# Seven block products for each pair of gate and up blocks in the second block's feed-forward

## Chip, cores and metric

The kernel runs on one core of one Trainium2 chip. The metric is the device time of one execution in microseconds. The time before is the median of three runs.

## What is computed

Two transformer blocks in float32 on 512 tokens (528 with meta tokens in the first block) of width 1024. The change touches the feed-forward of the second block (`d_model` 1024, inner width 2816):

```python
n2 = rmsnorm(h, g_ffn)
h = h + (jax.nn.silu(n2 @ w_ffn_gate) * (n2 @ w_ffn_up)) @ w_ffn_down
```

The factor 1/rms of a token multiplies a whole column of the transposed products, so the kernel applies it behind the products and only the gain `g_ffn` ahead of them.

## The kernel before

Activations are kept transposed: a row block is a tile of 128 features by 512 tokens, eight of them make the 1024 features. A weight block is 1024 x 128, kept as a tile of 128 x 8 x 128.

Every float32 operand of a matmul is split in two parts (high and low, tiles of type float32r), and a product is three matmuls: high by high, high by low, low by high (`mm`, L237 to L239; the weights' tiles are `wh` and `wl`). `load_w` (L218) loads a block from HBM into `wr` by SyncE's queue, copies it to `wh` on ScalarE (ACT, L226) and subtracts on VectorE (DVE, L228) for `wl`; each of these tags has three buffers (pool `wp`). `split` (L262) does the same for activations, and `gain_split` (L282) with the gain in it. `one` (L1327) computes one output block of 128 x 512 into a PSUM bank that `bank` (L245) picks: 8 x 3 matmuls of 128 x 512.

The end of `block2` (L1376 to L1452) runs in this order: eight output projections with residual (L1378 to L1383), `rstd` and the broadcast of 1/rms into `rsbc` (L1385 to L1387), eight gain splits (L1388), then three groups of inner blocks (8, 8 and 6, the loop at L1389). In a group each inner block j takes one gate and one up product; each is multiplied by `rsbc` out of PSUM (L1397, L1399), the gate goes through Silu (L1398), their product (L1400) is split (L1401). Then eight down projections (L1403) sum the group into the residual H. The ending (L1404 on) is the gate of a per-layer embedding and the final norm.

```python
nc.vector.tensor_tensor(g1, self.one(self.load_w(A["w_ffn_gate"][j]), X), rs_bc, OP.mult)
nc.scalar.activation(g1, g1, AF.Silu)
nc.vector.tensor_tensor(g2, self.one(self.load_w(A["w_ffn_up"][j]), X), rs_bc, OP.mult)
```

The order in which an engine gets its instructions is set by the tile framework's scheduler when the program is built; each engine then works its own list in order and waits on semaphores. A tag with n buffers lets the next tile in only when the readers of the n-th last are done. TensorE is PE below, with PEld its weight loads, GpSimd is POOL, SyncE is SP.

## Time and profile before

| what | value |
|---|---|
| median of 3 runs | 2286.45 us (2282.49 to 2290.6) |
| profiled execution, its own time | 2280.83 us |
| its span | 2279.0 us |
| mean granted clock of TensorE | 0.98 |
| PE busy | 2175.6 us (95%) |
| DVE, ACT, POOL busy | 1196.4, 918.6, 437.8 us |
| instructions: PE, DVE, ACT, POOL | 12395, 2045, 1544, 835 |

The profiled execution is one of the program's executions, its span the time from the first instruction to the last. Matmuls overlap in the pipeline, so PE's busy share alone tells little; the starts of successive matmuls and the waits between them do. The second block's feed-forward lies from about 1830 to 2222 us: gate and up products, the eight down projections of a group, and again.

### The profile page before, as it was taken

The page shows a single profiled execution, that of the slowest core. Times are in us where ns is not written, and L with a number is a line of the kernel's source. Part 1 is how long each engine was busy: PE and PEld are TensorE (multiplying, and loading weights), DVE is VectorE, ACT ScalarE, POOL GpSimd, SP SyncE. Part 2 cuts the span into 40 slices and gives each one's busy share as a digit, 9 for nine tenths or more (in the row PEclk, how much of TensorE's full clock was granted, in tenths as well). Part 3 has the DMA queues.
Part 4 walks back from the last instruction along what each step waited for, and adds up shares of the span by engine and source line. Part 5 has one row for each costly group of instructions (what it writes and reads, how often), then busy time and mean ns, then how long its engine had stood idle before and what let it go on. Part 6 is the DMA issues. An engine that isn't in the chain of part 4 may idle for free.

```text
span 2279.0 us, 31959 instructions
## 1 busy us (share of the span) xinstructions
PE 2175.6 (95%) x12395; PEld 1897.2 (83%) x12395; DVE 1196.4 (52%) x2045; ACT 918.6 (40%) x1544; POOL 437.8 (19%) x835
## 2 busy tenths in 40 slices
PE   6888899999999998899999999999999999999998
PEld 5887888999999977688888888788788888888887
DVE  4665667644434577653443465554554454344355
ACT  4554565323323476542332443343443332232233
POOL 4233431693000222100000002880000000000001
PEclk8899999999999999999999999999999999999999
DMA  4111232244342244232222236224223332222222
GB/s 148 58 48 29 64 108 83 101 130 151 110 123 93 84 74 96 62 133 97 93 93 99 96 111 144 80 82 123 100 89 96 127 114 93 102 93 93 99 91 88
DMA packets 105872, 221.93 MB, mean 97 GB/s; under 512 B 27812, under 2 KB 46361, under 8 KB 105720
## 3 DMA queue, kind: packets, MB, share of 16 engines
q1 hardware_dynamic: 105720, 219.88, 31.0%
q8 instruction: 98, 1.61, 0.3%
q14 instruction: 54, 0.44, 0.1%
HBM read 202.91 MB, written 15.57 MB: 96 GB/s over the span
## 4 chain that ended last, share of the span: by engine, by line
PE 86%; DVE 6%; ACT 3%; DMA 2%; issue 2%; POOL 1%; SPq 1%; DVEq 0%; ACTq 0%
PE mm L237 14%; PE mm L238 14%; PE mm L239 13%; PE x L237 10%; PE x L239 10%; PE x L238 10%; PE s L237 1%; PE s L238 1%; PE s L239 1%; PE s L662 1%; PE s L772 1%; PE t L390 1%; PE t L1042 1%; ACT wh L226 1%; PE s L1618 0%
## 5 line engine op out<-in xcount | busy, mean ns | idle before, releaser
L226 ACT ACTIVATE wh<-wr 128x1024 fp32r<-128x1024 f32 (+3 forms) x360 | 350.2, 974 | 1035.6 <-PE x L238 497.6
L228 DVE TENSOR_TENSOR wl<-wr,wh 128x1024 fp32r<-128x1024 f32 (+2 forms) x301 | 354.1, 1177 | 167.9 <-ACT wh L226 167.5
L237 PE MATMUL mm<-x,wh 128*128 128x512 f32 (+2 forms) x1144 | 409.8, 358 | 22.5 <-DVE raw L654 7.3
L238 PE MATMUL mm<-x,wh 128*128 128x512 f32 (+2 forms) x1144 | 404.3, 353 | 7.4 <-DVE x L287 7.4
L239 PE MATMUL mm<-x,wl 128*128 128x512 f32 (+2 forms) x1144 | 403.1, 352 | 0.0
L237 PEld LDWEIGHTS mm<-x,wh 128*128 128x128 f32 x1144 | 222.1, 194 | 52.8 <-ACT x L286 7.2
L237 PE MATMUL x<-x,wh 128*128 128x512 f32 (+1 forms) x728 | 258.3, 355 | 0.0
L239 PE MATMUL x<-x,wl 128*128 128x512 f32 (+1 forms) x728 | 257.4, 354 | 0.0
L238 PE MATMUL x<-x,wh 128*128 128x512 f32 (+1 forms) x728 | 257.1, 353 | 0.0
L238 PEld LDWEIGHTS mm<-x,wh 128*128 128x128 f32 x1144 | 221.7, 194 | 34.3 <-DVE x L287 8.5
L239 PEld LDWEIGHTS mm<-x,wl 128*128 128x128 f32 x1144 | 221.9, 194 | 28.1 <-issue 0.8
L228 POOL TENSOR_TENSOR wl<-wr,wh 128x1024 fp32r<-128x1024 f32 (+2 forms) x59 | 102.8, 1743 | 432.8 <-ACT wh L226 399.7
L237 PE MATMUL mm<-k,wh 128*128 128x272 f32 (+1 forms) x520 | 177.8, 342 | 1.2 <-ACT raw L892 0.5
L239 PE MATMUL mm<-k,wl 128*128 128x272 f32 (+1 forms) x520 | 176.4, 339 | 0.0
L238 PE MATMUL mm<-m,wh 128*128 128x272 f32 (+2 forms) x520 | 170.9, 329 | 5.7 <-DVE m L264 5.7
L239 PE MATMUL x<-k,wl 128*128 128x256 f32 (+1 forms) x520 | 174.3, 335 | 0.0
L237 PE MATMUL x<-k,wh 128*128 128x256 f32 (+1 forms) x520 | 173.6, 334 | 0.5 <-DVE h L880 0.5
L239 PEld LDWEIGHTS x<-x,wl 128*128 128x128 f32 x728 | 137.8, 189 | 20.1
L237 PEld LDWEIGHTS x<-x,wh 128*128 128x128 f32 x728 | 138.0, 190 | 19.5
L238 PEld LDWEIGHTS x<-x,wh 128*128 128x128 f32 x728 | 137.7, 189 | 19.8
L292 POOL TENSOR_TENSOR rs<-col,mhalf 128x5 f32<-128x5 f32 (+2 forms) x8 | 9.0, 1128 | 728.8 <-DVE col L304 728.8
L238 PE MATMUL x<-m,wh 128*128 128x256 f32 (+1 forms) x432 | 139.6, 323 | 0.1
(471 smaller groups left out, 3996.1 us busy)
## 6 DMA issues: line engine op xcount, KB each, us to landing
wr<-w_up SPq DMA_DIRECT2D x64, 512.0 KB, 3.3
wr<-w_down SPq DMA_DIRECT2D x64, 512.0 KB, 3.3
wr<-w_in SPq DMA_DIRECT2D x56, 512.0 KB, 3.2
wr<-w_ffn_gate SPq DMA_DIRECT2D x22, 512.0 KB, 3.3
wr<-w_ffn_up SPq DMA_DIRECT2D x22, 512.0 KB, 3.2
wr<-w_ine SPq DMA_DIRECT2D x18, 512.0 KB, 3.5
wr<-w_ffn_down SPq DMA_DIRECT2D x16, 512.0 KB, 3.3
wr<-w_ino SPq DMA_DIRECT2D x10, 512.0 KB, 3.2
```

Of the source, the lines that this page charges most:

```text
L226: nc.scalar.activation(wh, raw, AF.Copy)
L228: eng.tensor_tensor(wl, raw, wh.bitcast(F32), OP.subtract)
L237: self.nc.tensor.matmul(ps, wh[:, k0 + j], xh[:, a:b], start=start and j == 0, stop=False)
L238: self.nc.tensor.matmul(ps, wh[:, k0 + j], xl[:, a:b], start=False, stop=False)
L239: self.nc.tensor.matmul(ps, wl[:, k0 + j], xh[:, a:b], start=False, stop=stop and j == nk - 1)
L292: self.nc.gpsimd.tensor_tensor(dst, src, self.mhalf[:src.shape[0], :n], OP.pow)
L390: nc.tensor.transpose(t[:nk, b, :n], P[:n, k:k + nk], eye)
L662: nc.tensor.matmul(ps, v[:n, b], p[:n, b, :w], start=b == 0 and j == 0, stop=b == 4 and j == len(seq) - 1)
L772: self.nc.tensor.matmul(s[:, hf, :264], q, k[j][:, ks], start=j == 0, stop=j == 1)
L1042: nc.tensor.transpose(t[:, 128 * j:128 * j + 128], E[c][n][:, k:k + 128], self.turn)
```

## The change

Each pair of a gate block and an up block is now computed with a seven-product scheme for 2 x 2 block matrices (Strassen's, in the form with shared sums). The 2 x 2 blocks are: on the weights' side gate and up by even and odd K blocks (w11, w12 of the gate, w21, w22 of the up block), on the activations' side even and odd row blocks by the first and second 256 tokens. Each product has four K blocks and 256 columns: 4 x 3 matmuls of 128 x 256, into one half of a PSUM bank.

`seven_w` loads both blocks (the up block into the new tag `w2`), forms four sums of 128 x 512 on POOL into two tiles `ws`, and splits four tiles: the gate block, the two tiles of sums, and half of the up block. `seven_x` makes seven operands out of the eight row blocks with gain, once. `seven` runs the seven products and puts the results together on DVE, with two PSUM copies on ACT and one sum on POOL. The products with `rsbc` move from DVE (out of PSUM) to POOL (in SBUF). PSUM takes its banks from six in turn for the whole stage. The stage becomes a function `ffn` of its own, with a pool for the new tags (`x7` 8 buffers, `xo` 8, `ws` 3, `w2` 2, `st` 6).

```diff
@@ -227,6 +227,93 @@
         eng = nc.gpsimd if self.on_pool[self.nw % len(self.on_pool)] else nc.vector
         eng.tensor_tensor(wl, raw, wh.bitcast(F32), OP.subtract)
         return wh, wl
+
+
+    def seven_w(self, src1, src2):
+
+
+        nc = self.nc
+        self.n += 1
+        raws = self.wp.tile([128, 8, 128], F32, tag="wr", name=f"wr{self.n}", bufs=3), self.u("w2", F32, (128, 8, 128))
+        for raw, src in zip(raws, (src1, src2)):
+            nc.sync.dma_start(raw, src)
+        eo = lambda t: [t.rearrange("p (i e) n -> p e i n", e=2)[:, e] for e in range(2)]
+        (w11, w12), (w21, w22) = map(eo, raws)
+        s, r = self.u("ws", F32, (128, 8, 128)), self.u("ws", F32, (128, 8, 128))
+        G = nc.gpsimd
+        G.tensor_tensor(s[:, 0:4], w21, w22, OP.add)
+        G.tensor_tensor(s[:, 4:8], s[:, 0:4], w11, OP.add)
+        G.tensor_tensor(r[:, 0:4], w21, w11, OP.add)
+        G.tensor_tensor(r[:, 4:8], s[:, 4:8], w12, OP.add)
+        parts = []
+        for x, n in ((raws[0], 8), (s, 8), (r, 8), (w22, 4)):
+            self.n += 1
+            wh = self.wp.tile([128, 8, 128], F32R, tag="wh", name=f"wh{self.n}")
+            wl = self.wp.tile([128, 8, 128], F32R, tag="wl", name=f"wl{self.n}")
+            nc.scalar.activation(wh[:, :n], x, AF.Copy)
+            nc.vector.tensor_tensor(wl[:, :n], x, wh[:, :n].bitcast(F32), OP.subtract)
+            parts.append((wh, wl))
+        (ah, al), (sh, sl), (rh, rl), (dh, dl) = parts
+        (ah0, ah1), (al0, al1) = eo(ah), eo(al)
+        return ((ah0, al0), (ah1, al1), (sh[:, 0:4], sl[:, 0:4]), (sh[:, 4:8], sl[:, 4:8]),
+                (rh[:, 0:4], rl[:, 0:4]), (rh[:, 4:8], rl[:, 4:8]), (dh[:, 0:4], dl[:, 0:4]))
+
+    def seven_x(self, Z):
+
+
+        nc = self.nc
+        ops = [[] for _ in range(7)]
+        for i in range(4):
+            z0, z1 = Z(2 * i), Z(2 * i + 1)
+            A, B = slice(0, 256), slice(256, 512)
+            p, q = self.u("raw", F32, (128, 512)), self.u("raw", F32, (128, 512))
+            nc.vector.tensor_tensor(p[:, A], z0[:, A], z0[:, B], OP.subtract)
+            nc.vector.tensor_tensor(p[:, B], z1[:, B], z0[:, B], OP.subtract)
+            nc.vector.scalar_tensor_tensor(q[:, A], z1[:, B], -1.0, p[:, A], op0=OP.mult, op1=OP.subtract)
+            nc.vector.tensor_tensor(q[:, B], z1[:, A], q[:, A], OP.add)
+            h0, l0 = self.u("xo", F32R, (128, 256)), self.u("xo", F32R, (128, 256))
+            self.split(z0[:, A], h0, l0)
+            h1, l1 = self.split_new(z1, ("x", "x"))
+            hp, lp = self.split_new(p, ("x", "x"))
+            hq, lq = self.split_new(q, ("x7", "x7"))
+            for o, (h, l, c) in zip(ops, ((h0, l0, A), (h1, l1, A), (h1, l1, B), (hp, lp, A), (hq, lq, A), (hp, lp, B), (hq, lq, B))):
+                o.append((h[:, c], l[:, c]))
+        return ops
+
+    def seven(self, W, X, o1, o2):
+
+        nc = self.nc
+        w11, w12, s1, s2, r1, r2, w22 = W
+        b11, b21, b22, t1, t2, t3, t4 = X
+        A, B = slice(0, 256), slice(256, 512)
+
+        G = nc.gpsimd
+
+        def prod(w, x):
+            ps = self.bank()[:, A]
+            for j, (xh, xl) in enumerate(x):
+                nc.tensor.matmul(ps, w[0][:, j], xh, start=j == 0, stop=False)
+                nc.tensor.matmul(ps, w[0][:, j], xl, start=False, stop=False)
+                nc.tensor.matmul(ps, w[1][:, j], xh, start=False, stop=j == 3)
+            return ps
+
+        def new(ps=None):
+            t = self.u("st", F32, (128, 256))
+            if ps is not None:
+                nc.scalar.activation(t, ps, AF.Copy)
+            return t
+
+        v1 = new(prod(w11, b11))
+        nc.vector.tensor_tensor(o1[:, A], prod(w12, b21), v1, OP.add)
+        v2 = new()
+        nc.vector.tensor_tensor(v2, prod(s2, t2), v1, OP.add)
+        c5 = new(prod(s1, t1))
+        v3 = new()
+        nc.vector.tensor_tensor(v3, prod(r1, t3), v2, OP.add)
+        G.tensor_tensor(v2, v2, c5, OP.add)
+        nc.vector.scalar_tensor_tensor(o2[:, B], c5, -1.0, v3, op0=OP.mult, op1=OP.subtract)
+        nc.vector.tensor_tensor(o2[:, A], prod(w22, t4), v3, OP.subtract)
+        nc.vector.tensor_tensor(o1[:, B], prod(r2, b22), v2, OP.add)
 
     def mm(self, ps, w, xs, sl, ks=None, k0=0, start=True, stop=True):
 
@@ -1381,22 +1468,31 @@
             nc.vector.tensor_tensor(h, self.one(self.load_w(A["w_out"][m]), mix), x, OP.add)
             self.sq_add(acc, h, m == 0, (0, 512))
             H.append(h)
+        return H, acc
+
+    def ffn(self, H, acc):
+        nc, A = self.nc, self.A
 
         rs = self.rstd(acc, 1024, BLOCKS2)
         rs_bc = self.u("rsbc", F32, (128, 512))
         self.bcast(rs_bc, rs, BLOCKS2)
-        X = [self.gain_split(H[m], self.g(C_GF, m), (0, 512)) for m in range(8)]
+
+        def z(m):
+            t = self.u("q", F32, (128, 512))
+            nc.scalar.activation(t, H[m], AF.Copy, scale=self.g(C_GF, m))
+            return t
+
+        self.banks(6)
+        X = self.seven_x(z)
         for a, b, wd in ((0, 8, lambda m: A["w_ffn_down0"][0, m]), (8, 16, lambda m: A["w_ffn_down0"][1, m]),
                          (16, 22, lambda m: A["w_ffn_down1"][0, m])):
             S = []
             for j in range(a, b):
-                if j in (0, 2):
-                    self.banks(2 if j else 6)
-                g1, g2 = self.u("raw"), self.u("raw")
-                g1, g2 = g1[:, :512], g2[:, :512]
-                nc.vector.tensor_tensor(g1, self.one(self.load_w(A["w_ffn_gate"][j]), X), rs_bc, OP.mult)
+                g1, g2 = self.u("raw")[:, :512], self.u("raw")[:, :512]
+                self.seven(self.seven_w(A["w_ffn_gate"][j], A["w_ffn_up"][j]), X, g1, g2)
+                nc.gpsimd.tensor_tensor(g1, g1, rs_bc, OP.mult)
                 nc.scalar.activation(g1, g1, AF.Silu)
-                nc.vector.tensor_tensor(g2, self.one(self.load_w(A["w_ffn_up"][j]), X), rs_bc, OP.mult)
+                nc.gpsimd.tensor_tensor(g2, g2, rs_bc, OP.mult)
                 nc.vector.tensor_tensor(g1, g1, g2, OP.mult)
                 S.append(self.split_new(g1, ("k", "h")))
             for m in range(8):
@@ -1654,7 +1750,9 @@
                 return
             st.callback(self.inner.__exit__, None, None, None)
             with self.pool({"o2": 3, "pd": 2, "pf": 2, "dmask": 1}):
-                self.block2(*got)
+                got = self.block2(*got)
+            with self.pool({"x7": 8, "xo": 8, "ws": 3, "w2": 2, "st": 6}):
+                self.ffn(*got)
 
     def pool(self, tags):
         return self.sb.open(self.tc, tags)
```

**Order, the inner blocks.** DVE, one pair before the change (`raw` are the two results, `k` and `h` the split of the product, `mm` and `x` PSUM banks):

```order
L1397 TENSOR_TENSOR raw_19083<-mm_19091,rsbc_18068 128x512
L228 TENSOR_TENSOR wl_19192<-wr_19190,wh_19191 128x1024
L1399 TENSOR_TENSOR raw_19084<-x_19124,rsbc_18068 128x512
L1400 TENSOR_TENSOR raw_19083<-raw_19083,raw_19084 128x512
L228 TENSOR_TENSOR wl_19231<-wr_19229,wh_19230 128x1024
L264 TENSOR_TENSOR h_19152<-raw_19083,k_19151 128x512
```

DVE now, one period of a pair in the middle of a group. `wl<-ws` and `wl<-w` are low parts of the sums and of the up block's half, `wl<-wr` of the gate block of the pair after; `s`, `mm` and `x` are PSUM banks, `st` SBUF tiles:

```order
L254 TENSOR_TENSOR wl_18900<-ws_18889,wh_18899 128x1024
L316 TENSOR_TENSOR raw_18743<-s_18861,st_18800 128x256
L351 TENSOR_TENSOR h_18740<-raw_18603,k_18739 128x512
L254 TENSOR_TENSOR wl_18904<-ws_18890,wh_18903 128x1024
L307 TENSOR_TENSOR raw_18883<-mm_18926,st_18924 128x256
L254 TENSOR_TENSOR wl_18908<-w_18886,wh_18907 128x512
L309 TENSOR_TENSOR st_18940<-x_18941,st_18924 128x256
L254 TENSOR_TENSOR wl_19036<-wr_19025,wh_19035 128x1024
L312 TENSOR_TENSOR st_18970<-s_18971,st_18940 128x256
L1496 TENSOR_TENSOR raw_18743<-raw_18743,raw_18744 128x512
L314 SCALAR_TENSOR_TENSOR raw_18884<-st_18968,st_18970 128x256
L315 TENSOR_TENSOR raw_18884<-s_18987,st_18970 128x256
```

Six instructions became twelve; seven of the twelve read two SBUF tiles, five read a PSUM bank and an SBUF tile. The two that read PSUM and `rsbc` are gone.

**Order, POOL.** Before, POOL's list between the scan of the state-space part and the ending:

```order
L1505 TENSOR_TENSOR st_14638<-a_5053,vh_14000 64x32 x2
L1506 TENSOR_TENSOR st_14637<-st_14637,vh_14000 128x32
L1507 TENSOR_TENSOR vh_14000<-st_14637,st_14638 128x32
L292 TENSOR_TENSOR rs_18066<-col_18064,mhalf 128x4
L1431 TENSOR_SCALAR m_17795<-m_17795,cols 128x512
L1431 TENSOR_SCALAR m_17833<-m_17833,cols 128x512
```

The row of L292 is the 1/rms; nothing stands between it and the ending. POOL now, one period of a pair (`ws<-` are the four sums for a later pair, L1495 and L1493 the products with `rsbc` of an earlier pair, L313 a sum of the current one):

```order
L244 TENSOR_TENSOR ws_19169<-w_19166 128x512
L313 TENSOR_TENSOR st_18940<-st_18940,st_18968 128x256
L245 TENSOR_TENSOR ws_19169<-ws_19169,wr_19165 128x512
L1495 TENSOR_TENSOR raw_18884<-raw_18884,rsbc_18072 128x512
L246 TENSOR_TENSOR ws_19170<-w_19166,wr_19165 128x512
L247 TENSOR_TENSOR ws_19170<-ws_19169,wr_19165 128x512
L1493 TENSOR_TENSOR raw_18883<-raw_18883,rsbc_18072 128x512
```

Seven instructions per pair are new on this engine. Right behind these rows comes the end of the first group:

```order
L244 TENSOR_TENSOR ws_19565<-w_19562 128x512
L313 TENSOR_TENSOR st_19080<-st_19080,st_19108 128x256
L1495 TENSOR_TENSOR raw_19024<-raw_19024,rsbc_18072 128x512
L1493 TENSOR_TENSOR raw_19023<-raw_19023,rsbc_18072 128x512
L313 TENSOR_TENSOR st_19220<-st_19220,st_19248 128x256
L1495 TENSOR_TENSOR raw_19164<-raw_19164,rsbc_18072 128x512
L1493 TENSOR_TENSOR raw_19163<-raw_19163,rsbc_18072 128x512
L245 TENSOR_TENSOR ws_19565<-ws_19565,wr_19561 128x512
L246 TENSOR_TENSOR ws_19566<-w_19562,wr_19561 128x512
L244 TENSOR_TENSOR ws_19705<-w_19702 128x512
L247 TENSOR_TENSOR ws_19566<-ws_19565,wr_19561 128x512
```

The first row is a sum for the next group's first pair; the six behind it finish the group's last two pairs; from L245 on stand the rest of the eight sums for the next group's first two pairs. Eight such sums also stand ahead of the first group.

## Rows read from the trace of the kernel before

**Rows 1.** The page, chain that ended last: share of the span by engine.

```profile
PE 86%; DVE 6%; ACT 3%; DMA 2%; issue 2%; POOL 1%; SPq 1%; DVEq 0%; ACTq 0%
```

**Rows 2.** Busy us per engine, two stretches; PEclk, DMA share, GB/s.

```profile
core 0: us, PE busy (x) PEld busy (x) DVE busy (x) ACT busy (x) POOL busy (x), PEclk, DMA share, GB/s
627.00:684.00 57.00, 57.00 (x471) 56.91 (x470) 22.32 (x32) 14.06 (x16) 0.00 (x0) 1.00 0.41 121
1995.00:2052.00 57.00, 57.00 (x249) 46.56 (x248) 26.77 (x32) 17.70 (x22) 0.00 (x0) 1.00 0.27 93
```

**Rows 3.** PE's waits, 1830 to 2200 us: total us, times, longest us.

```profile
PE mm L237 <- DVE m L1403: 0.3, 1, 0.3
```

**Rows 4.** Timeline of PE (start us, us, instruction): first and last of 22.

```profile
1989.71 0.40 PE L239 MATMUL mm<-x,wl 128*128 128x512 f32 x1
...
1994.54 0.39 PE L239 MATMUL mm<-x,wl 128*128 128x512 f32 x1
```

**Rows 5.** Timeline of PE at 256 columns: first and last of 24.

```profile
743.75 0.28 PE L237 MATMUL x<-k,wh 128*128 128x256 f32 x1
...
746.46 0.28 PE L239 MATMUL x<-k,wl 128*128 128x256 f32 x1
```

**Rows 6.** DVE groups, 1760:2210 us: count, busy us, mean ns, idle before.

```profile
L228 DVE TENSOR_TENSOR wl<-wr,wh 128x1024 fp32r<-128x1024 f32 x72 | 88.1, 1223 | 19.6 <-ACT wh L226 19.5
L1400 DVE TENSOR_TENSOR raw<-raw,raw 128x512 f32<-128x512 f32 x22 | 15.2, 692 | 2.6 <-ACT raw L1398 0.7
L287 DVE SCALAR_TENSOR_TENSOR x<-m,cols,x 128x512 fp32r<-128x512 f32 x8 | 6.0, 746 | 0.0
L228 DVE TENSOR_TENSOR wl<-wr,wh 128x512 fp32r<-128x512 f32 x8 | 5.4, 681 | 0.0
```

**Rows 7.** ACT groups, same stretch.

```profile
L226 ACT ACTIVATE wh<-wr 128x1024 fp32r<-128x1024 f32 x72 | 76.4, 1061 | 248.2 <-PE mm L238 119.7 <-issue 80.8 <-PE x L238 43.6
L226 ACT ACTIVATE wh<-wr 128x512 fp32r<-128x512 f32 x7 | 4.4, 633 | 20.8 <-PE mm L238 12.4 <-PE x L238 8.4
```

**Rows 8.** POOL: one of 512 (timeline); four of 256 (ns min/median/max).

```profile
184.87 1.27 POOL L228 TENSOR_TENSOR wl<-wr,wh 128x512 fp32r<-128x512 f32 x1 [4.76 <-ACT wh L226]
...
L1449 POOL TENSOR_TENSOR k<-m,rsbc x4: 723/725/910, 2268.2 to 2273.2; 128x256 f32<-128x256 f32 x4
```

**Rows 9.** Timeline of DVE near the start.

```profile
8.92 0.77 DVE L287 SCALAR_TENSOR_TENSOR x<-m,cols,x 128x528 fp32r<-128x528 f32 x1 [0.41 <-ACT x L286]
9.61 0.70 DVE L512 TENSOR_TENSOR acc<-acc,raw 128x528 f32<-128x528 f32 x1
...
15.44 2.88 DVE L512 TENSOR_TENSOR acc<-acc,raw 128x528 f32<-128x528 f32 x1
18.24 2.84 DVE L287 SCALAR_TENSOR_TENSOR x<-m,cols,x 128x528 fp32r<-128x528 f32 x1
```

**Rows 10.** Timeline of POOL, same time: two of 1024 in one row.

```profile
14.99 5.53 POOL L228 TENSOR_TENSOR wl<-wr,wh 128x1024 fp32r<-128x1024 f32 x2
```

**Rows 11.** Timeline of DVE at 456 us.

```profile
456.41 0.42 DVE L1139 TENSOR_TENSOR h<-x,h 128x256 f32<-128x256 f32 x1 [2.38 <-PE x L239]
457.39 1.41 DVE L228 TENSOR_TENSOR wl<-wr,wh 128x1024 fp32r<-128x1024 f32 x1 [0.55 <-ACT wh L226]
```

**Rows 12.** Timeline of POOL, same time.

```profile
456.17 0.43 POOL L1243 TENSOR_TENSOR p<-p,p 128x128 f32<-128x128 f32 x1
...
457.29 0.43 POOL L1242 TENSOR_TENSOR p<-p,p 128x128 f32<-128x128 f32 x1
457.67 1.41 POOL L1243 TENSOR_TENSOR p<-p,p 128x128 f32<-128x128 f32 x1
```

**Rows 13.** A wait of PE; the stretch behind it (columns as rows 2).

```profile
1380.13 2.10 PE L1496 MATMUL s<-u,sw 128*128 128x64 f32 x10 [1.77 <-issue]
1380.20:1390.00 9.80, 9.80 (x40) 9.12 (x41) 3.18 (x4) 4.40 (x5) 0.00 (x0) 0.51 0.45 139
```

**Rows 14.** Timeline of DVE, output projections.

```profile
1827.84 0.69 DVE L1381 TENSOR_TENSOR m<-mm,raw 128x512 f32<-128x512 f32 x1 [2.13 <-PE mm L239]
```

## Prediction

> **What bounds the kernel now.** I read the chain of waits first: TensorE's matmuls make up 86% of what ended last [rows 1]. Then the busy time by stretch: in a stretch of gate and up projections (from 1995 us) PE is busy all 57 us at a granted clock of 1.00, while DVE is busy 26.77, ACT 17.70 and POOL 0.00 [rows 2]. Then PE's waits in the whole feed-forward stage of the second block: one, of 0.3 us [rows 3]. So this stage costs what its matmuls cost, and a change here is worth its matmuls only as long as no other engine becomes later than PE.
>
> The timeline gives the spacing of matmuls: 512 columns, 22 starts from 1989.71 to 1994.54, so 4.83/21 = 0.230 us [rows 4]; 256 columns, 24 starts from 743.75 to 746.46, so 2.71/23 = 0.118 us [rows 5]. PEld's records fill all of the stretch from 627 us, where 272 and 256 columns alternate [rows 2]; its loads are thus in that spacing already.
>
> **The change, part by part.** A pair is one gate block and one up block; there are 22.
>
> *Matmuls.* Removed per pair: 2 x 8 x 3 = 48 of 512 columns, 48 x 0.230 = 11.04 us. Added: 7 x 4 x 3 = 84 of 256 columns, 84 x 0.118 = 9.91 us. Alone that is -1.13 us a pair, -24.9 us in all.
> The page "TensorE: Matmul & The Clock Gate" of the Trainium skill (section "Back-to-back issue gap") speaks against such a trade: about 81 ns per matmul at 128 columns and 131 ns at 512 in a stream with weight loads. By a straight line between them, an estimate, 256 columns would take 98 ns, the pair 8.2 us in place of 6.3, and the stage 42 us more. The rows here show 0.118 and 0.230, nearly a half, and the measurement decides.
>
> *ACT* gets per pair 3 x 1.06 + 0.63 for the wh tiles [rows 7], two PSUM copies, a Silu and a split, none over 0.63: under 6.4 us, less than PE's 9.91, hidden by it. The DMAs carry the same bytes as before.
>
> *DVE* gets per pair twelve instructions. Seven read two SBUF tensors: three wl of 1024 elements (1.22 each), one of 512 (0.68), the product of gate and up (0.69), a split (0.69 at most) [rows 6] and the 256-wide L314 (about 0.42, as the 256-wide row of rows 11). That is 6.14 us. Five read PSUM, 0.42 each [rows 11]. Together 8.2 us: alone it would fit under 9.91.
>
> *POOL*, idle in this stage before, gets six instructions of 512 (1.27 each) and one of 256 (0.73) [rows 8]: 8.35 us. Alone it would fit too.
>
> *Together they don't fit.* At the start of the program a DVE instruction on 528 elements takes 0.70 or 0.77, but 2.88 and 2.84 while POOL runs two instructions of 1024 [rows 9, 10]. Subtract the usual length from the end: the first DVE row came through at 18.32 - 0.70 = 17.62, the second at 21.08 - 0.77 = 20.31. At 456 us it goes the other way: POOL's row at 457.67 takes 1.41 instead of 0.43, that is, it came through at 458.65, and the DVE row beside it, 1.41 instead of 1.22, at 457.58 [rows 11, 12]. One waits until the other is done. So a DVE instruction of 1024 elements holds POOL up for 458.65 - 457.58 = 1.07 us, and (528 elements: 0.55) POOL's 1024 hold DVE up from 18.17 to 20.31, 2.14 us. The DVE row at 456.41, which reads PSUM and one SBUF tensor, takes 0.42 in the middle of POOL's stream: it doesn't take part.
> The page "SBUF — State Buffer" of the Trainium skill (section "Who interferes with whom") says the same of a DVE instruction with two SBUF inputs and a GpSimd one that reads SBUF, and that the one that starts first keeps the port pair for its whole instruction. The rows agree on who waits, but show a hold a little shorter than the record. By the page's words the sum is nearer the upper bound below, by the rows nearer the lower one.
>
> The price per pair. Lower bound, holds end to end: POOL 6 x 1.07 + 0.54 = 6.96; DVE 3 x 1.07 + 3 x 0.54 + 0.27 = 5.10; 12.1 us. Upper bound, whole records end to end: 8.35 + 6.14 = 14.5 us. Both are over 11.04. I take 13.0, nearer the lower end, because the contested rows go by holds; the 0.9 above it is for moments in which one engine waits for data rather than for the other.
>
> PE has no slack to absorb this. The wh and wl tags have three buffers and a pair now takes four tiles: the next pair's second tile (in the order: raw gate block, s, r, half of the up block) gets the buffer of this pair's third, which the seventh product reads last. From that product's end ACT (1.06) and DVE (1.22) have 24 x 0.118 = 2.83 us, the next pair's first two products, to make it: 0.55 us to spare. One POOL instruction of 512 in front of that subtraction (1.07) uses it up, and the PSUM evictions queue behind it on DVE.
>
> Not every pair pays. The sums for the first pairs of a down-projection group are formed while the down projections or the output projection run (POOL has nothing else there), and beside the last two pairs of a group POOL forms hardly any sums for a following pair (its order, shown above with the change, has one sum of the next group there). I let two pairs in each of the three groups run at PE's 9.91: 6 x (9.91 - 11.04) = -6.8. The other 16: 16 x (13.0 - 11.04) = +31.4; bounds 16 x 1.06 = +17 and 16 x 3.46 = +55.
>
> *Operands.* The eight gain splits (DVE 8 x 0.75 = 6.0 [rows 6]) become 20 instructions of 256 (0.42) and 12 of 512 (0.69): 16.7 us of DVE, in four equal steps. Three steps lie beside the output projections, where DVE sits idle 2.13 us before an eviction [rows 14]; the last needs the last row block: 4.2 us against one split of 0.75 before. I take +4; bounds 0 and 16.7 - 6.0 = +10.7.
>
> Sum: -6.8 + 31.4 + 4 = **+28.6 us**. The profiled execution took 2280.83 us (span 2279.0) and would go to 2309; it lies 5.6 under the median of the runs shown, 2286.45, so the median would be **2315 us**. A difference under 0.3%, 7 us, can't be told from none by a measurement of this kernel.
>
> **The rivals.**
> *The port doesn't bind; PE does.* Then the stage gains 24.9 and loses 4 at the start: 2265 us. For it: each engine alone is under 9.91. Against: rows 9 to 12; it needs the port work to fall under 9.9 us a pair, and the lower bound is 12.1.
> *A draw.* If far more of the sums fall into the down projections than I grant, so that the 16 pairs average about 11.2, the result is 16 x 0.16 - 6.8 + 4 = 0: 2286. Against: ws has three buffers, one and a half pairs.
> *The clock falls as well.* Behind a PE wait of 1.77 us the granted clock averaged 0.51 over 10 us [rows 13], that is, it stood at 1.2 GHz nearly all the time, where the gate and up products have 2.4 GHz, 1.00 [rows 2]. A wait of about 3 us in each pair could do that 16 times. Much of the slower time lies under the same port work, so I price it with the port's upper bound: 55 - 6.8 + 10.7 = +59, 2345 us; a drop that isn't covered adds to that.
>
> **How the numbers follow.** Forecast 0.70; clock and upper bound 0.11; PE bound 0.11; a draw 0.08. The port's bounds with those of the operands give 17 - 6.8 + 0 = +10 to +59, 2296 to 2345. To hold 8 in 10 I go from 2290, within the draw, to 2348, and leave out the gain and the far end of the clock case. Slower by over 0.3%: 0.70 + 0.11 = 0.81; within: 0.08; faster: 0.11.
>
> **What would show it.** Right: 36 more matmuls per pair, 0.118 apart while they run; POOL's 512-wide records at about 2 us instead of 1.27 and DVE's wl at about 2 instead of 1.22; PE idle two to three us per pair, put down to DVE wl L254, some 45 us over the stage; the gate and up stretches longer, the down stretches the same. Wrong: PE busy throughout the pairs and DVE and POOL at their usual lengths (the gain came), or a 256-wide spacing well over 0.118 with no wait (the matmuls or the clock were the cause).

## The result and the profile after

| kernel | median us (lowest to highest) | ratio to before, 95% interval |
|---|---|---|
| before | 2284.47 (2278.04 to 2290.60, 4 runs) | |
| changed | 2315.45 (2303.09 to 2320.19, 4 runs) | 1.0128 [1.0079, 1.0177] |

The kernel became slower by 1.3%; 2315 was forecast. The profiled execution took 2320.19 us. The page, busy time and the chain that ended last [rows 1]:

```profile
PE 2170.4 (94%) x13187; PEld 1928.5 (83%) x13187; DVE 1361.1 (59%) x2201; ACT 972.7 (42%) x1648; POOL 690.4 (30%) x989
...
PE 75%; DVE 10%; POOL 5%; ACT 3%; DMA 3%; issue 3%; SPq 1%; DVEq 0%; ACTq 0%; POOLq 0%
```

PE's share of the chain fell from 86 to 75%; DVE and POOL gained 8 points. By the shares of busy time alone nothing seems short: DVE is busy 59% of the span and POOL 30%. The stage tells more. PE's waits in the second block's feed-forward (1810 to 2260 us; line and releaser, total us, times, longest), where one wait of 0.3 us had been [rows 3]:

```profile
PE s L297 <- DVE wl L254: 25.2, 17, 2.4
PE mm L297 <- DVE wl L254: 6.3, 4, 2.5
PE x L297 <- DVE wl L254: 3.3, 3, 1.2
```

All 34.8 us are waits for the low part of a weight tile, in 24 places. Busy time over the first five spacings of the second group, a spacing running from one pair's last eviction to the next pair's (columns as rows 2):

```profile
2026.52:2091.33 64.81, 56.36 (x432) 54.47 (x431) 58.40 (x59) 27.15 (x41) 57.96 (x35) 0.95 0.26 82
```

A pair takes 64.81/5 = 12.96 us there, in place of 11.04; that is a mean of 14.16, 10.47, 13.66, 14.14 and 12.38. DVE is busy 58.40 us of it, POOL 57.96, about 11.6 us a pair each, where their own work is 8.2 and 8.35. The groups of the same stretch (count, busy us, mean ns) show where the rest comes from; DVE, against rows 6 and 11:

```profile
L254 DVE TENSOR_TENSOR wl<-ws,wh 128x1024 fp32r<-128x1024 f32 x10 | 20.6, 2062 | 0.0
L254 DVE TENSOR_TENSOR wl<-wr,wh 128x1024 fp32r<-128x1024 f32 x5 | 9.8, 1968 | 0.0
L254 DVE TENSOR_TENSOR wl<-w,wh 128x512 fp32r<-128x512 f32 x5 | 7.2, 1439 | 0.0
...
L1496 DVE TENSOR_TENSOR raw<-raw,raw 128x512 f32<-128x512 f32 x5 | 4.8, 950 | 4.5 <-ACT raw L1494 4.5
...
L315 DVE TENSOR_TENSOR raw<-s,st 128x256 f32<-128x256 f32 x3 | 1.2, 409 | 0.0
```

POOL, against rows 8:

```profile
L1493 POOL TENSOR_TENSOR raw<-raw,rsbc 128x512 f32<-128x512 f32 x5 | 10.3, 2059 | 0.0
L246 POOL TENSOR_TENSOR ws<-w,wr 128x512 f32<-128x512 f32 x5 | 10.3, 2053 | 0.0
...
L313 POOL TENSOR_TENSOR st<-st,st 128x256 f32<-128x256 f32 x5 | 7.3, 1452 | 0.0
L245 POOL TENSOR_TENSOR ws<-ws,wr 128x512 f32<-128x512 f32 x5 | 7.0, 1392 | 0.1
L244 POOL TENSOR_TENSOR ws<-w 128x512 f32<-128x512 f32 x5 | 6.6, 1313 | 6.8 <-DMA w<-w_ffn_up 5.2 <-DVE raw L1496 1.5
```

DVE's low parts went from 1.22 to 2.06 and 1.97 us and from 0.68 to 1.44; POOL's 512-wide rows from 1.27 to as much as 2.06. DVE's instructions that read a PSUM bank and one SBUF tile stayed at 0.41. One such moment, in DVE's timeline (start, us, instruction):

```profile
1920.38 1.96 DVE L254 TENSOR_TENSOR wl<-ws,wh 128x1024 fp32r<-128x1024 f32 x1
```

in PE's (in brackets the idle time before it and what ended it):

```profile
1919.61 0.28 PE L296 MATMUL x<-x,wh 128*128 128x256 f32 x1
1922.39 0.39 PE L297 MATMUL mm<-x,wl 128*128 128x256 f32 x1 [2.50 <-DVE wl L254]
1922.61 0.28 PE L295 MATMUL mm<-x,wh 128*128 128x256 f32 x1
```

and the clock behind it (columns as rows 2):

```profile
1923.00:1926.50 3.50, 3.50 (x21) 3.50 (x20) 3.50 (x3) 0.50 (x1) 3.50 (x3) 0.56 0.00 0
```

The subtraction ended at 1922.34 and PE went on at 1922.39, 2.50 us late. A microsecond later the granted clock stood at 1.2 GHz for some 3.4 us. In half-microsecond slices there are five such falls in the stage, each 0.4 to 1.4 us behind a wait of 1.75 to 2.50 us; they cost 8.5 us of full-speed time together. Not every such wait has one behind it: one of 2.13 us, which ended at 1908.08, has none. The stage before has no fall.

**Length of the stage**, from the start of the first output-projection eviction to that of the last down eviction: 402.6 us before (1819.53 to 2222.1), 430.0 after (from 1831.75 to the second row here, DVE's timeline):

```profile
1831.75 0.69 DVE L1468 TENSOR_TENSOR m<-mm,raw 128x512 f32<-128x512 f32 x1 [4.04 <-PE mm L326]
...
2261.75 0.69 DVE L1499 TENSOR_TENSOR m<-s,m 128x512 f32<-128x512 f32 x1 [1.41 <-PE s L326]
```

So the stage grew by 27.4 us. The two profiled executions are 39.4 us apart: the stage starts 12.2 us later, after unchanged code (last section), and 0.2 come back behind it. The experiments are therefore read by the stage and the spacing of pairs beside the ratio.

### The profile page after: what moved, and what is told of

Read it like the earlier page. It is cut to its first block, busy times and chain, and to the rows that moved or that the text cites. A ratio compares the mean times of both kernels' runs of the same rounds, so it can differ in the third digit from the quotient of the medians.

```text
span 2318.4 us, 34040 instructions
## 1 busy us (share of the span) xinstructions
PE 2170.4 (94%) x13187; PEld 1928.5 (83%) x13187; DVE 1361.1 (59%) x2201; ACT 972.7 (42%) x1648; POOL 690.4 (30%) x989
## 4 chain that ended last, share of the span: by engine, by line
PE 75%; DVE 10%; POOL 5%; ACT 3%; DMA 3%; issue 3%; SPq 1%; DVEq 0%; ACTq 0%; POOLq 0%
PE mm L324 11%; PE mm L325 11%; PE mm L326 11%; PE x L325 8%; PE x L324 8%; PE x L326 8%; PE s L324 2%; PE s L325 2%; PE s L326 2%; DVE wl L254 2%; PE s L749 1%; PE s L859 1%; PE t L477 1%; DVE wl L228 1%; DMA w<-w_ffn_up 1%
## 5 line engine op out<-in xcount | busy, mean ns | idle before, releaser
L226 ACT ACTIVATE wh<-wr 128x1024 fp32r<-128x1024 f32 (+3 forms) x316 | 303.1, 961 | 838.4 <-PE x L325 469.1
L228 DVE TENSOR_TENSOR wl<-wr,wh 128x1024 fp32r<-128x1024 f32 (+2 forms) x257 | 323.2, 1259 | 156.9 <-ACT wh L226 156.0
L324 PE MATMUL mm<-x,wh 128*128 128x512 f32 (+2 forms) x976 | 344.8, 353 | 31.4 <-DVE h L1226 8.3
L325 PE MATMUL mm<-x,wh 128*128 128x512 f32 (+2 forms) x976 | 338.7, 347 | 7.4 <-DVE x L374 7.4
L326 PE MATMUL mm<-x,wl 128*128 128x512 f32 (+2 forms) x976 | 337.4, 346 | 0.0
L324 PEld LDWEIGHTS mm<-x,wh 128*128 128x128 f32 x976 | 191.0, 196 | 55.1 <-DVE h L1226 8.5
L325 PEld LDWEIGHTS mm<-x,wh 128*128 128x128 f32 x976 | 191.0, 196 | 27.1 <-DVE x L374 8.5
L326 PEld LDWEIGHTS mm<-x,wl 128*128 128x128 f32 x976 | 190.8, 195 | 20.8 <-issue 0.8
L324 PE MATMUL x<-x,wh 128*128 128x512 f32 (+1 forms) x560 | 192.6, 344 | 0.0
L325 PE MATMUL x<-x,wh 128*128 128x512 f32 (+1 forms) x560 | 191.6, 342 | 0.0
L326 PE MATMUL x<-x,wl 128*128 128x512 f32 (+1 forms) x560 | 191.6, 342 | 0.0
L297 PE MATMUL s<-x,wl 128*128 128x256 f32 x352 | 103.0, 297 | 25.3 <-DVE wl L254 25.2
L326 PEld LDWEIGHTS x<-x,wl 128*128 128x128 f32 x560 | 106.5, 190 | 12.9
```

The lines of the kernel that those rows point to most:

```text
L226: nc.scalar.activation(wh, raw, AF.Copy)
L228: eng.tensor_tensor(wl, raw, wh.bitcast(F32), OP.subtract)
L297: nc.tensor.matmul(ps, w[1][:, j], xh, start=False, stop=j == 3)
L324: self.nc.tensor.matmul(ps, wh[:, k0 + j], xh[:, a:b], start=start and j == 0, stop=False)
L325: self.nc.tensor.matmul(ps, wh[:, k0 + j], xl[:, a:b], start=False, stop=False)
L326: self.nc.tensor.matmul(ps, wl[:, k0 + j], xh[:, a:b], start=False, stop=stop and j == nk - 1)
```

## The experiments

"Pair" is the spacing of the last product's evictions (`prod(r2, b22)`) in the middle of the second group, "stage" as above; both are read from the one profiled execution of each kernel. A ratio is to runs of the kernel before made beside that row's runs; their medians lie between 2277.81 and 2286.42 us, so the ratios and not the medians compare from row to row.

| kernel | pair, us | stage, us | median, us | ratio to before, 95% |
|---|---|---|---|---|
| before | 11.0 | 402.6 | | |
| changed | 12.96 | 430.0 | 2315.45 | 1.0128 [1.0079, 1.0177] |
| e1_no_rms_product | 12.0 | 408.7 | 2282.52 | 1.0019 [0.9999, 1.0038] |
| e2_sum_twice | 13.9 | 441.3 | 2314.39 | 1.0160 [1.0138, 1.0183] |
| e5_own_buffers | 12.9 | 420.5 | 2302.18 | 1.0088 [1.0062, 1.0115] |
| e8_scaled_operands | 12.0 | 427.1 | 2307.71 | 1.0125 [1.0105, 1.0145] |
| e10_no_rms_own_buffers | 10.9 | 389.0 | 2262.66 | 0.9927 [0.9904, 0.9951] |
| e13_c5_from_psum | 12.0 | 404.2 | 2282.76 | 1.0027 [1.0003, 1.0051] |
| e11_scaled_steps | 10.9 | 409.5 | 2284.43 | 1.0032 [1.0009, 1.0055] |
| e12_all_three | 10.3 | 401.2 | 2277.07 | 0.9985 [0.9958, 1.0012] |
| e14_scale_in_down | 11.9 | 396.5 | 2272.71 | 0.9968 [0.9942, 0.9994] |
| e15_and_one_sum_on_dve | 11.8 | 398.9 | 2273.99 | 0.9972 [0.9948, 0.9996] |
| e16_two_sums_on_dve | 12.1 | 405.2 | 2286.10 | 1.0020 [0.9994, 1.0047] |
| e17_scale_split | 10.3 | 393.2 | 2274.58 | 0.9948 [0.9919, 0.9976] |

**e1_no_rms_product.**

```diff
-                nc.gpsimd.tensor_tensor(g1, g1, rs_bc, OP.mult)
                 nc.scalar.activation(g1, g1, AF.Silu)
-                nc.gpsimd.tensor_tensor(g2, g2, rs_bc, OP.mult)
```

> Leaves out the two products with 1/rms on POOL (L1493, L1495), so gate and up go into the Silu unscaled; everything else is the changed kernel. The stage is taken from the start of the first output-projection eviction to that of the last down eviction: 402.6 us before, 430.1 after. Theory (DVE and POOL exclude each other): two instructions of 512 leave the shared work, 12.1 - 2 x 1.07 = 10.0 us a pair by holds, about PE's 9.91. The stage falls by 35 to 48 us (16 pairs by 2.1 to 3.0), to 382 to 395, PE's waits for DVE's wl from 34.8 us to under 10, ratio to the kernel before 0.99 to 0.995. Rival, the three wh/wl buffers are the cause: these products release no weight tile, so the stage falls by 5 us at most and the waits stay over 25 us. Rival, the clock: the stretches at 1.2 GHz stay and the waits with them.

The stage fell by 21.3 us, more than the buffers' rival allows and less than the theory's 35 to 48: a pair went to 12.0 and not to 10. PE's waits for wl fell to 24.7 us only, where under 10 was expected; the longest is now 1.7 us, and the clock doesn't fall in the stage. The timelines show what held it there, POOL's first:

```profile
1991.28 1.29 POOL L244 TENSOR_TENSOR ws<-w 128x512 f32<-128x512 f32 x1 [8.85 <-DMA w<-w_ffn_up]
...
2004.35 1.85 POOL L244 TENSOR_TENSOR ws<-w 128x512 f32<-128x512 f32 x1 [5.18 <-DMA w<-w_ffn_up]
2006.17 0.73 POOL L313 TENSOR_TENSOR st<-st,st 128x256 f32<-128x256 f32 x1
```

and DVE's:

```profile
1999.98 0.67 DVE L254 TENSOR_TENSOR wl<-w,wh 128x512 fp32r<-128x512 f32 x1
...
2006.94 0.42 DVE L316 TENSOR_TENSOR raw<-s,st 128x256 f32<-128x256 f32 x1 [1.88 <-POOL st L313]
```

DVE's low part of the up block's half ends at 2000.65 and frees that block's tile; the next up block lands 3.7 us later, at 2004.35; POOL's sum of it stands ahead of L313, which the current pair needs; DVE waits 1.88 us at L316 for that, with its next low parts behind. A ring through the buffers lies right behind the first limit.

**e2_sum_twice.**

```diff
         G.tensor_tensor(r[:, 4:8], s[:, 4:8], w12, OP.add)
+        G.tensor_tensor(r[:, 4:8], s[:, 4:8], w12, OP.add)
```

> The last of the four sums on POOL (L247) is done twice, so one more POOL instruction of 512 per pair, the same data. POOL alone would then have 9.6 us a pair, still under PE's 9.91. Theory (exclusion): the hold of 1.07 us is added to each pair in which the sums lie beside the pairs, 16 to 22 of them: the stage grows by 17 to 24 us to 447 to 454, ratio to the kernel before 1.02 to 1.024. Rival, the three wh/wl buffers or the clock are the cause and POOL's length isn't: under 5 us, 430 to 435.

A pair grew by 0.9 us, near the hold of 1.07, the stage by 11.3 and not by 17 to 24. The same view as above for five pairs:

```profile
2025.83:2095.39 69.56, 55.94 (x420) 53.22 (x420) 61.98 (x61) 26.43 (x40) 69.41 (x41) 0.95 0.24 76
```

POOL is now busy 69.41 of 69.56 us. In the changed kernel it had 6.85 us idle in its five pairs; the added instruction filled these first, 1.3 us a pair, which is why 2.3 us more of POOL's busy time lengthened a pair by 0.9 only. POOL's own work would be 9.6 of these 13.9 us, so the other 4.3 are spent held off by DVE.

**e5_own_buffers.**

```diff
+            if n == 4:
+                wh, wl = (self.u("q", F32R, (128, 4, 128)) for _ in range(2))
```

> The parts of the up block's half (128x512) get tiles of another tag (four buffers that are free in this stage), so that a pair takes three wh/wl tiles and not four: the next pair's second tile waits for this pair's fourth product and no longer for its seventh. The work on all engines is unchanged. Theory (exclusion sets the rate, the buffers only where the wait shows): the shared work per pair stays 12.1 to 14.5 us, the stage falls by 0 to 10 us, to 420 to 430, and PE still waits 25 us or more, perhaps on other instructions. Rival (the buffers are the cause, each engine alone has under 9.91): the waits fall under 8 us, the stage to 380 to 392, ratio under 0.99.

The stage fell by 9.5 us, the waits for wl came to 27.5. The pairs in the middle didn't change, 12.89 us; the last two of the first two groups fell to about 9.1 and 8.5, those of the third to 7.0 and 8.8. The buffers are thus not what sets the pace of a pair; they matter for the ring of e1_no_rms_product and for the catching up at a group's end. At the start the edit costs: the first pair's last eviction comes 59.1 us after the first output-projection eviction, in place of 50.4 in the changed kernel, with five low parts in DVE's list between that pair's first eviction and its last in place of three. The tag `q`, taken for free in this stage, also holds the operands' row blocks (`z`) at its start; whether that is the reason was not tried. The later runs with own buffers have this too (55.6 to 59.1 us). Four pairs:

```profile
2026.40:2077.96 51.56, 42.31 (x336) 41.48 (x336) 51.56 (x49) 21.38 (x32) 46.92 (x28) 0.97 0.26 82
```

DVE is busy all 51.56 us, 12.9 a pair, of which 8.2 are its own. With buffers enough, the limit is **DVE's list**: its own work and the time that POOL holds it off.

**e8_scaled_operands.**

```diff
+        def zs(m):
+            t = self.u("q", F32, (128, 512))
+            nc.vector.scalar_tensor_tensor(t, H[m], self.g(C_GF, m), rs_bc, op0=OP.mult, op1=OP.mult)
+            return t
...
-                nc.gpsimd.tensor_tensor(g1, g1, rs_bc, OP.mult)
+                if a == 0:
+                    nc.gpsimd.tensor_tensor(g1, g1, rs_bc, OP.mult)
+                    nc.gpsimd.tensor_tensor(g2, g2, rs_bc, OP.mult)
                 nc.scalar.activation(g1, g1, AF.Silu)
-                nc.gpsimd.tensor_tensor(g2, g2, rs_bc, OP.mult)
...
+            if a == 0:
+                X = self.seven_x(zs)
             for m in range(8):
```

> During the first group's down projections the seven operands are made anew with 1/rms in them (DVE, one instruction with two factors per row block); the second and third group then need no product with 1/rms on POOL. The first group is as in the changed kernel. DVE gets 22.7 us beside 44 us of down projections in which it is busy some 15. Theory (exclusion): 14 pairs in groups two and three have 10.0 us of shared work in place of 12.1; about 10 to 12 of them were paying, 2.1 to 3.0 us each: the stage falls by 21 to 36 us, to 394 to 409, ratio to the kernel before 0.995 to 1.005, and the waits for wl lie in the first group. Rival (buffers or clock): no gain, 428 to 440, since DVE's added work can only cost.

Only 2.9 us came. Groups two and three ran at 12.0, as in e1_no_rms_product, and took 13.3 us less than in the changed kernel; from the first output-projection eviction to the second group's first pair it took 10.4 us more, 7.7 of them over the down projections beside which DVE now makes the operands. Alone this settles nothing.

**e10_no_rms_own_buffers** (the edits of the first and the third run, the two diffs above).

> Both edits of the first two runs together: the two products with 1/rms are left out (gate and up go unscaled into the Silu) and the parts of the up block's half get tiles of their own. Without the products alone, pairs came every 12.0 us with POOL idle for 5 us of each: there POOL's first sum waited for the up block's transfer (8.85 us), that transfer for DVE's low part of the half block, and DVE for POOL's sum L313 behind it (1.88 us). Theory (two limits: the exclusion, and behind it this ring through the buffers): with own buffers alone a pair took 12.9 us; two instructions less leave 12.9 - 2 x 1.07 = 10.8 us by that and 10.0 by holds, the stage 383 to 393 us, ratio to the kernel before 0.983 to 0.991. Rival, the ring does not go through these buffers: pairs stay at 11.5 to 12.0, the stage over 398. Rival, the exclusion was never the limit: then pairs stay at 12.0 as well, and the PE waits are on something other than wl.

10.94 us a pair, 389.0 the stage: both limits are real, and each hides the other's gain. Without POOL's two products alone a pair won 1.0, with own buffers alone 0.1, with both 2.0. Four pairs:

```profile
2009.35:2053.12 43.77, 42.20 (x353) 41.57 (x351) 43.77 (x49) 21.59 (x32) 29.35 (x20) 1.00 0.30 97
```

DVE is still busy the whole time, but POOL only 29.35 of it: the two instructions of 512 that POOL lost took 2 x 0.98 us out of DVE's list, on which they never stood. DVE has the same instructions in both runs (49 in four pairs) and no idle time in either, so the gain can't be a wait for data that the two products had caused.

**e13_c5_from_psum.**

```diff
-        c5 = new(prod(s1, t1))
+        c5 = prod(s1, t1)
...
-        G.tensor_tensor(v2, v2, c5, OP.add)
+        nc.vector.tensor_tensor(v2, c5, v2, OP.add)
```

> Own buffers as in e5_own_buffers, and the fifth product is read by DVE out of its PSUM bank, twice, instead of being copied by ACT; the sum L313 goes from POOL to DVE. POOL loses one instruction of 256 (hold 0.54), L314 leaves the shared work (0.27), DVE gets 0.42 more that reads PSUM. Theory (exclusion): 0.81 us a pair, 12.9 to 12.1, in 15 to 22 pairs: the stage falls from 420.5 by 12 to 18 us, to 402 to 409. Rival (DVE standing in order behind POOL's L313 is what costs): the whole wait of some 2 us a pair goes, the stage to 375 to 390. Rival (PSUM banks held longer stop PE): PE waits for DVE's raw or st, the stage over 415.

12.0 a pair and 404.2, as the theory had it: DVE got one more instruction and its list became 0.9 us shorter, because that instruction and the next, L314, now read PSUM and the hold of POOL's sum is gone. PE now waits 12.5 us for PSUM banks (raw L317); the gain was not lost by that.

**e11_scaled_steps** (`seven_step` is one round of the loop in `seven_x`).

```diff
             for m in range(8):
+                if a == 0 and m % 2 == 0:
+                    self.seven_step(m // 2, zs, X)
```

> Own buffers, and 1/rms put into the operands during the first group's down projections, now a step of two row blocks ahead of each second down projection and not all at once (the stretch over those projections took 61.8 us in e8_scaled_operands against 54.9 in the other group). Theory: first group as with own buffers alone (12.9 us a pair), the other two at 10.0 to 10.8, the transition under 57 us: the stage 390 to 400, ratio to the kernel before 0.988 to 0.996. Rival (ring or exclusion as in the rivals of e10_no_rms_own_buffers): groups two and three at 12.0, the stage over 405.

The pairs came as expected, 10.9; the stage is 9.5 us over the range, since the transition still took 60.4 us and the first group kept 12.9.

**e12_all_three** (that and the edit of e13_c5_from_psum).

> Everything of e11_scaled_steps, and the fifth product read out of PSUM as in e13_c5_from_psum. Shared work by holds 12.1 - 0.8 = 11.3 us a pair in the first group and 9.2 in the others, so that there PE's 9.91 is the bound. Theory: 12.1 a pair in the first group, 9.9 to 10.2 in the others, the stage 378 to 390, ratio to the kernel before 0.980 to 0.991. Rival (banks held longer, or the ring): pairs over 11 in groups two and three, no gain on e11_scaled_steps.

10.3 in groups two and three, 401.2 the stage, 11 us over the range: the seven products break even with the kernel before, and no more, since from the last output-projection eviction to the second group's first pair it takes 13.3 us longer than before.

**e14_scale_in_down** (e13_c5_from_psum, and `t` from `raw`).

```diff
-                nc.gpsimd.tensor_tensor(g2, g2, rs_bc, OP.mult)
...
+                nc.vector.tensor_tensor(t, self.one(self.load_w(wd(m), b - a), S), rs_bc, OP.mult)
+                nc.vector.tensor_tensor(H[m], t, H[m], OP.add)
```

> As e13_c5_from_psum, and the up block's product with 1/rms moves from the pairs (POOL, SBUF) to the evictions of the down projections: DVE multiplies the PSUM bank by 1/rms and adds the residual in a second instruction, beside projections in which it idles 3.4 us each. Theory (exclusion): one hold of 1.07 us less a pair, 12.0 to 10.9; the stage falls from 404.2 by 14 to 18 us less 1 to 3 for the longer evictions, to 387 to 393, ratio to the kernel before 0.993 to 0.997. Rival (the ring through PSUM banks or buffers decides now): pairs at 11.5 or more, the stage over 396.

A gain, but half of it: 11.2 us a pair in the first group, 11.9 in the others. Waits in four pairs of the second group:

```profile
DVE raw L1498 <- ACT raw L1497: 6.0, 4, 1.5
POOL raw L1496 <- DVE raw L319: 3.8, 4, 1.0
```

DVE stands 1.5 us in each pair at the product of gate and up, for the Silu, which waits for POOL's product with 1/rms, which waits for DVE's own last eviction; the scheduler put L1498 close behind that eviction. The changed kernel has the same stop (L1496 above: 4.5 us in five pairs). Without it a pair would still not come to 11.9 - 1.5 = 10.4 us: in three pairs of the first group DVE has no idle time, and they take 11.2 each.

```profile
1885.36:1919.09 33.73, 31.01 (x261) 30.66 (x260) 33.73 (x40) 15.90 (x22) 27.11 (x15) 1.00 0.29 94
```

**e15_and_one_sum_on_dve** and **e16_two_sums_on_dve** (the first on top of e14_scale_in_down, the second of e13_c5_from_psum; the line of w21 + w22 in the second alone).

```diff
-        G.tensor_tensor(s[:, 0:4], w21, w22, OP.add)
+        nc.vector.tensor_tensor(s[:, 0:4], w21, w22, OP.add)
...
-        G.tensor_tensor(r[:, 0:4], w21, w11, OP.add)
+        nc.vector.tensor_tensor(r[:, 0:4], w21, w11, OP.add)
```

> As e14_scale_in_down, and one of the four weight sums (w21 + w11) moves from POOL to DVE, where its hold is 0.54 in place of 1.07. DVE's own time goes to about 9.3 us a pair. Theory (exclusion): 10.9 to 10.4 us a pair, close to PE's 9.91 with the 0.4 us that e12_all_three kept above it; the stage 380 to 388, ratio to the kernel before 0.989 to 0.994. Rival (DVE becomes the bound in order, the sum waiting for transfers ahead of evictions): no gain on e14_scale_in_down or a loss, PE waiting for DVE's raw.

> As e13_c5_from_psum, with both products with 1/rms left on POOL, and two of the four weight sums (w21 + w22, w21 + w11) moved to DVE. Work is not removed, only moved from the engine that holds longer to the one that holds 0.54. Theory (exclusion): 2 x (1.07 - 0.54) = 1.06 us less a pair, 12.0 to 10.9; the stage 387 to 394, ratio to the kernel before 0.993 to 0.998. Rival (POOL's own pace is the limit, no exclusion): POOL gets 2 x 1.27 less, DVE has 10.0 of its own, pairs at 10.0 to 10.2, the stage 378 to 384. Rival (DVE's pace is): DVE gets 1.4 us more, pairs at 13.4, the stage over 420.

Both miss: no gain, 11.8 and 12.1. Three pairs of e16_two_sums_on_dve:

```profile
2030.43:2066.68 36.25, 29.95 (x243) 28.77 (x242) 36.25 (x46) 15.04 (x21) 22.02 (x13) 1.00 0.27 88
```

POOL is busy only 22.02 of 36.25 us, so neither its pace nor the sum of all holds is the limit; DVE's list is full. A sum moved to DVE adds its 0.68 there and takes away at most a hold of 1.07. In my sum of holds it counted as a gain of 0.53; measured, the two moved sums gave back no more than the 0.68 that each cost. I take it that part of a hold passes while DVE works on PSUM banks, which no run shows by itself. The sum of holds is a lower bound, not the price.

**e17_scale_split** (e12_all_three, and in the first group the edit of e14_scale_in_down, with POOL adding the residual; the first group's product of `g2` with `rs_bc` goes).

```diff
+                if a == 0:
+                    t = self.u("raw")[:, :512]
+                    nc.vector.tensor_tensor(t, ps, rs_bc, OP.mult)
+                    nc.gpsimd.tensor_tensor(H[m], t, H[m], OP.add)
+                else:
+                    nc.vector.tensor_tensor(H[m], ps, H[m], OP.add)
```

> As e12_all_three (groups two and three without any product with 1/rms, pairs at 10.3 us there), and in the first group the up block's product with 1/rms moves from POOL to the evictions of the down projections: DVE multiplies the PSUM bank by 1/rms, POOL adds the residual. Theory (exclusion in the first group): 12.0 to about 11 us for its pairs, as the first group of e14_scale_in_down had (69.3 us from the first pair's end to the eighth's against 80.7), the transition up to 2 us longer: the stage falls from 401.2 by 7 to 11 us, to 390 to 394, ratio to the kernel before 0.993 to 0.997. Rival (DVE is full in the transition, 22.7 us of operands beside the longer evictions): the transition grows by what the pairs win, the stage at 398 or more.

393.2 us, 0.9948 [0.9919, 0.9976]: 0.5% faster than the kernel before. Four pairs of the second group, and from that group's end to the last down eviction:

```profile
2021.40:2062.68 41.28, 40.65 (x336) 39.83 (x336) 41.14 (x54) 20.07 (x28) 25.53 (x16) 1.00 0.31 103
...
2078.30:2215.85 137.55, 137.55 (x843) 123.10 (x842) 89.36 (x118) 50.42 (x66) 34.20 (x23) 1.00 0.32 101
```

PE is busy 40.65 of 41.28 us. In the third group the matmuls' gain is whole: from the second group's last pair to the last down eviction 137.1 us against 144.3, 7.2 less, where 6 pairs x 1.13 = 6.8 was to be had, and PE never stops in it. The evictions of a pair still come 10.3 us apart while PE's 504 matmuls of that group start from 2122.60 to 2182.32, 9.97 us a pair: DVE falls behind and catches up at the group's end, so the spacing of evictions overstates what a pair costs. Over the whole stage 9.4 of the 24.9 us show: the first pair's last eviction comes 5.9 us later than before, counted from the first output-projection eviction, and the first group, from there to its last pair, takes as long as before (73.9 us against 74.0).

## Why the prediction was right

- **Matmuls.** Right: in the changed kernel 19 starts from 2182.72 to 2184.84, 0.118 us apart. The 1.13 us a pair were there; e17_scale_split collects them in its third group.
- **Exclusion of DVE and POOL.** Right, and shown by taking POOL's instructions away (e10_no_rms_own_buffers against e5_own_buffers: 0.98 us of DVE's time for each of 512) and by adding one (0.9). The Trainium skill's page "SBUF — State Buffer", section "Who interferes with whom", exempts a DVE instruction with at most one SBUF input; the trace agrees (0.41 in the middle of POOL's work), and e13_c5_from_psum gains by it.
- **13.0 us a pair.** Measured 12.96 over five spacings, but that agreement is luck: one of the five is a cheap one, and 13.0 was meant for the dear ones. What I called waiting for data is there: DVE is idle 1.3 us a pair, 0.9 of it for the Silu.
- **Sixteen paying pairs and six cheap ones.** The count is right, the places are not all: of the 19 spacings within groups six are 10.2 to 11.1 us, the others 13.5 on average. The cheap ones are the last of the first two groups, the last two of the third, and the second of groups two and three; none reaches 9.91.
- **Operands +4.** Too much: from the first output-projection eviction to the first pair's last it is 50.4 us in place of 51.7, 1.3 less, about the pair's own 1.13, and from 1840 to 1890 us PE waits 0.2 us only. The operands delayed nothing there; in the runs with own buffers that stretch is longer.
- **Sum +28.6.** The stage: +27.4. Two misses offset each other: without the 1.3 us at the start the pairs cost 28.7 in place of 31.4 - 6.8 = 24.6, and the operands 1.3 less than nothing in place of 4. That the median came within half a microsecond of 2315 is luck on top of that: the median before, on which the forecast stands, came out 2 us lower, the four executions lie 17 us apart, and the profiled one holds 12.2 us from code that the change doesn't touch.
- **PE idle some 45 us.** 34.8 in waits, and in the five spacings above PE is idle (64.81 - 56.36)/5 = 1.7 us a pair, not two to three. The loss to explain is 27.4 + 24.9 = 52.3; 8.5 more went into the clock's falls. Of the other 9 some 6 belong to the same waits, by an estimate from the rows above: a wait is counted from the end of the matmul's record, but from start to start (1919.61, 1922.39, 1922.61) the one of 2.50 us took 3.00 - 2 x 0.118 = 2.76, 0.26 more, and there are 24. About 3 I can't assign.
- **The clock.** I gave it to a rival as one more cost. It fell five times, each time behind a wait for wl, and is part of the same 27.4: it comes with the waits for DVE and not beside them. In the stage of e10_no_rms_own_buffers, where no wait for wl is over 0.8 us, it doesn't fall; in that of e1_no_rms_product, with waits of up to 1.7, it doesn't either.
- **What I had too simple**: that the holds of both engines add up to one shared resource. They lengthen DVE's list, and a second limit (the ring through the up block's buffer) stood right behind. I also put PE's lack of slack down to the three wh and wl buffers; with own buffers the pairs in the middle stayed at 12.89 us, so more slack would not have absorbed DVE's longer list. None of this changed the forecast; it changed what the first experiments gave.

## What to carry to other kernels

Moving work to an idle engine isn't free when its instructions and those of the engine that feeds PE hold each other off: count each of its instructions at about 1 us per 512 elements on the other engine's list as well (0.98 by taking two away), unless that engine reads PSUM at the time. Moving such an instruction to the full engine gave no gain here. Look at busy engines by pair and not by span, and expect a second limit behind the first: take away both at once in one run before calling a suspect cleared. Read the pace of PE from its own matmuls: evictions can fall behind it and catch up. Fewer matmuls paid here only once the extra element-wise work had been moved out of the loop (into the operands and the down evictions) or onto PSUM.

## What was not expected of the hardware

Ahead of the stage, in code that is the same in both kernels, DVE lost far more than one hold. The changed kernel's timeline of DVE:

```profile
484.65 13.09 DVE L228 TENSOR_TENSOR wl<-wr,wh 128x1024 fp32r<-128x1024 f32 x1 [0.55 <-ACT wh L226]
```

of POOL, two of the last rows of a stream:

```profile
496.10 0.46 POOL L1333 TENSOR_TENSOR p<-p,p 128x128 f32<-128x128 f32 x1
496.51 1.53 POOL L1332 TENSOR_TENSOR p<-p,p 128x128 f32<-128x128 f32 x1
```

and PE's waits from 480 to 510 us:

```profile
PE mm L324 <- DVE h L1226: 8.3, 1, 8.3
```

A DVE subtraction that takes 1.22 us stood for 13.09, through 29 POOL instructions of 0.41 to 0.46 us from 485.17 to 496.10, each of which began after it. Only the one at 496.51 waited (1.53 = 0.46 + 1.07, DVE's hold). In the trace of before no DVE instruction from 450 to 500 us took over 1.54 us. So in a stream of short POOL instructions DVE doesn't always get the next turn.

The eviction behind it starts at 497.66 us, in the trace of before at 484.44: 13.2 us later, where the one of rows 11, at 456.41 before, had started 0.8 us earlier, at 455.60. With another long DVE record in between (8.04 us at 469.07) this place makes up the 12.2 us by which the stage starts later. From 493.3 to 503.5 us the granted clock was 0.50. Of the 14 traces nine have a DVE instruction of over 6 us at this place and five have none, and variants of the changed kernel are among both. With one trace of each kernel it isn't shown whether executions of the same kernel differ in this way; what decides it was not tried.
